# Loading w_mod first, three of its row tiles in full fp32, and the rest of it on Pool's queue

## The chip, the cores and the metric

The kernel runs on one core of one Trainium2 chip. The metric is the time of one execution in microseconds, as the device reports it. Before the change it is 1837.02 us, the median of three runs (1834.33 to 1839.08).

## The reference, cut to what matters

One layer of a diffusion backbone over 1024 latent tokens and 256 context tokens of width 1024. Per sample, a conditioning vector gives six vectors of modulation; the tokens are normalised, scaled and shifted, and projected by one large matrix:

```python
def adaln_params(cond, w_mod, b_mod):
    m = jax.nn.silu(cond) @ w_mod + b_mod            # (1024,) @ (1024, 6144)
    return jnp.split(m[..., None, :], N_MOD, axis=-1)
...
    sh1, sc1, g1, sh2, sc2, g2 = adaln_params(c, w_mod[l], b_mod[l])
    csh1, csc1, cg1, csh2, csc2, cg2 = adaln_params(c_ctx, w_mod[l], b_mod[l])
    hx = modulate(rms_norm(x, norm1_g[l]), sh1, sc1)       # h * (1 + scale) + shift
    hc = modulate(rms_norm(ctx, norm1_g[l]), csh1, csc1)
    y_x, y_c = token_mix(hx, hc, w_in[l], ...)             # begins with hx @ w_in and hc @ w_in
    x = x + g1 * y_x
    x = x + g2 * expert_choice_moe(modulate(rms_norm(x, norm2_g[l]), sh2, sc2), ...)
```

Token mixing (a recurrent branch, an attention branch, gates) and sixteen experts follow. All data are fp32.

## The kernel before, in words

**Precision.** Most products are made of three matmuls in the type fp32r, which keeps fewer bits of a number: an operand is written as `hi` (rounded by ACT, `nc.scalar.copy`, line 92) and `lo` (the rest, subtracted by DVE, line 93), and hi*hi + hi*lo + lo*hi are summed (`mm3g`, lines 172 to 179). `split` is this pair of instructions.

**The opening stage (lines 242 to 369)** computes shift and scale of the first norm and modulates the tokens. The first 2048 of w_mod's 6144 columns come in eight row tiles `wm` of 128 x 2048 (1 MB); `silu(c)` and `silu(c_ctx)` stand in columns, `s_col`, and as hi and lo in `s4` (four columns). For each tile k: split into `w2` (ACT, then DVE), then eight matmuls of 512 columns into four sums `pm` (line 322). Then the sums are copied to `m2`, turned into columns (`ptc`, line 339), and with b_mod and norm1_g become `modc` and the scale `sv` (lines 342 to 345).

Beside that the ten token tiles (0 and 1 are context; 2 to 5 are half 0 of x, 6 to 9 half 1) are loaded (`xload`), normalised (`normalise`: ACT squares and sums, Pool computes the inverse root, lines 85 and 87, DVE or Pool multiplies, line 296 or 294) and turned by PE (`turn_in`, line 303; DVE and ACT copy the result, line 304). The tuples XA, XB, XC say behind which tile k a token tile is loaded, normalised and turned; 9 means behind the loop. `modulate` multiplies and adds per row of channels (line 350; DVE for even k, Pool for odd) and splits the result into HC (context) and HX[0], HX[1] (the halves).

**The projection.** `ws` is a stream of w_in's column tiles of 256 columns (`wload`, lines 156 to 166: load to `raw`, split into `whi` and `wlo`); two of them can stand ready. `natural` multiplies one column tile by the token tiles asked for, 24 matmuls of 256 columns each (lines 176 to 178), and ACT copies each result to `stg` (three buffers), from which SP's queue stores it (`staged`, line 70). In the opening stage column 0 is multiplied with tiles 0 and 1, then with 2 to 4 (XD = 3) with the turns of half 1 between them, and behind the modulation of half 1 with 5 to 9. Columns 1 to 20 follow. The remaining 4096 columns of w_mod are loaded in sixteen tiles of 1 MB (line 490, two buffers) and summed by DVE, each times its number of `s_col` (`macc`, lines 493 and 495); this is written in the loop over columns 3 to 6, and the scheduler moves it up to columns 0 to 3. The sums end in a product in plain fp32 (line 518), whose result is needed much later.

**What sets the order.** PE executes in the order in which the program is written. For the other engines a scheduler orders instructions by priority; each engine then executes its queue strictly in order, and a waiting instruction holds all behind it. DMAs are instructions of the engine that issues them (SP, ACT or Pool) and wait in its queue for the buffers that they fill. Buffers are shared by tag: before, the eight w_mod tiles go round the four buffers whi0, wlo0, whi1, wlo1.

Of the kernel before, what the change touches and what calls it, by code (L numbers as in the profile page):

```python
# [9 lines left out]
F32 = mybir.dt.float32  # L10
F32R = mybir.dt.float32r
# [10 lines left out]
D = 1024  # L22
# [12 lines left out]
def dram(a, off, dims):  # L35
    return bass.AP(tensor=a.tensor, offset=a.offset + off, ap=[list(d) for d in dims])
# [9 lines left out]
def _layer(tc, nc, top, A, out):  # L46
# [43 lines left out]
    def split(hi, lo, src, eng=None):  # L90

        nc.scalar.copy(hi, src)  # L92
        (eng or nc.vector).tensor_tensor(lo, src, hi.bitcast(F32), op=OP.subtract)  # L93
# [93 lines left out]
    hxp = top.enter_context(ExitStack())  # L187
    hx_pool = hxp.enter_context(mkpool(name="hx", bufs=1))

    HX = [[hx_pool.tile([128, 8, 512], F32R, name="hx", tag=f"hx0{i}") for i in range(2)]]  # L190
    hcp = top.enter_context(ExitStack())
    hc_pool = hcp.enter_context(mkpool("right", name="hc", bufs=1))
    HC = [hc_pool.tile([128, 8, CT], F32R, name=f"hc{i}") for i in range(2)]
# [11 lines left out]
    def natural(hi, lo, emit, tiles):  # L205

        n = hi.shape[2]
        for t in tiles:
            h = HC if t < 2 else HX[(t - 2) // 4]
            o = (t if t < 2 else (t - 2) % 4) * 128  # L210
            p = pjt()
            yield from mm3g(p[:, :n], (lambda k: h[0][:, k, o:o + 128], lambda k: h[1][:, k, o:o + 128]),
                            (lambda k: hi[:, k], lambda k: lo[:, k]), 8)
            emit(t, p[:, :n])
            fill.flushed()
# [11 lines left out]
    def dense(gen):  # L227
        for _ in gen:
            pass
# [12 lines left out]
    with ExitStack() as st:  # L242
# [5 lines left out]
        X = {}  # L248

        def xload(t):  # L250
            X[t] = pool.tile([128, D], F32, name="xt", tag="xt", bufs=4)
            nc.sync.dma_start(X[t], A["ctx"][0, t * 128:(t + 1) * 128] if t < 2 else A["x"][0, (t - 2) * 128:(t - 1) * 128])


        XA, XB, XC = (0, 0, 1, 1, 2, 2, 9, 9, 9, 9), (1, 1, 2, 2, 3, 4, 9, 9, 9, 9), (2, 3, 4, 5, 6, 6, 9, 9, 9, 9)
        XD = 3
        wm = []
        for k in range(8):
            w = wp.tile([128, 2048], F32, name="wm", tag=("whi0", "wlo0", "whi1", "wlo1")[k % 4])
            nc.sync.dma_start(w, dram(A["w_mod"], k * 128 * 6144, [[6144, 128], [1, 2048]]))  # L260
            wm.append(w)
            for t in range(10):
                if XA[t] == k:
                    xload(t)
        n1 = pool.tile([8, 128], F32, name="n1")
        nc.scalar.dma_start(n1, A["norm1_g"].rearrange("a (k p) -> (a k) p", p=128))
        bm = pool.tile([16, 128], F32, name="bm")
# [15 lines left out]
        nc.vector.tensor_copy(n1c, pt[:, 16:40])  # L283

        XN = {}
        MP, NP = (1, 3, 5, 7), (1, 3, 5, 7, 9)

        def normalise(t):
            ss = pool.tile([128, 1], F32, name="ss", bufs=3)
            scr = pool.tile([128, D], F32, name="scr", tag="scr", bufs=2)  # L290
            nc.scalar.activation(scr, X[t], AF.Square, accum_out=ss)
            r = rsqrt(pool, ss, 1, 1.0 / D, "rx")
            if t in NP:
                nc.gpsimd.tensor_scalar(scr, X[t], r, 1.0, op0=OP.mult, op1=OP.mult)
            else:
                nc.vector.tensor_scalar(scr, X[t], r, None, op0=OP.mult)
            XN[t] = scr
# [13 lines left out]
        def turn_in(t):  # L311
            if t < 2:
                transpose_in(t, xnc, t * 128)
            else:
                transpose_in(t, halves[(t - 2) // 4], (t - 2) % 4 * 128)

        for k in range(8):
            w2 = hx_pool.tile([128, 2, 2048], F32R, name="wm2", tag="hx1%d" % (k % 2))
            split(w2[:, 0], w2[:, 1], wm[k])
            for j in range(4):  # L320
                for i in range(2):
                    nc.tensor.matmul(pm[j], s4[:, k], w2[:, i, j * 512:(j + 1) * 512],
                                     start=(k == 0 and i == 0), stop=(k == 7 and i == 1))
            for t in range(10):
                if XB[t] == k:
                    normalise(t)
                if XC[t] == k:
                    turn_in(t)
        HX.append([hx_pool.tile([128, 8, 512], F32R, name="hx", tag=f"hx1{i}") for i in range(2)])
        ws.load(0)  # L330
        for t in range(10):
            if XA[t] > 7:
                xload(t)
        m2 = pool.tile([4, 2048], F32, name="m2")
        for j in range(4):
            (nc.scalar.copy if j % 2 else nc.vector.tensor_copy)(m2[:, j * 512:(j + 1) * 512], pm[j])
        pc = ps.tile([128, 512], F32, name="ptc", tag="tp", bufs=2)
        for j in range(16):
# [5 lines left out]
        sv = pool.tile([128, 8, 2], F32, name="sv")  # L344
        nc.vector.scalar_tensor_tensor(sv, modc[:, 8:], 1.0, n1c[:, :8, None].to_broadcast([128, 8, 2]),
                                       op0=OP.add, op1=OP.mult)

        def modulate(xt, dst, o, n, j):
            for k in range(8):
                (nc.gpsimd if k in MP else nc.vector).tensor_scalar(xt[:, k], xt[:, k], sv[:, k, j:j + 1], modc[:, k, j:j + 1], op0=OP.mult, op1=OP.add)  # L350
                split(dst[0][:, k, o:o + n], dst[1][:, k, o:o + n], xt[:, k])

        modulate(xnc, HC, 0, CT, 1)
        for t in range(10):
            if XB[t] > 7:
                normalise(t)
        for t in range(6):
            if XC[t] > 7:
                turn_in(t)
        (w,), ahead = ws.next()  # L360
        dense(natural(*w, to_v(0), range(2)))
        modulate(halves[0], HX[0], 0, 512, 0)
        for t in range(2, 6):
            if t - 2 < XD:
                dense(natural(*w, to_v(0), [t]))
# [23 lines left out]
    with ExitStack() as st:  # L389
# [26 lines left out]
        for i, n in enumerate(("c_cos", "c_sin")):  # L416
            a = pool.tile([128, 8, 64], F32, name="rot", bufs=1, tag="rot%d" % i)
            nc.scalar.dma_start(a, A[n].rearrange("(t p) c -> p t c", p=128))
            (nc.gpsimd, nc.vector)[i].tensor_tensor(a, a, rows[:, i:i + 1].to_broadcast([128, 8, 64]), op=OP.mult)
            rot.append(a)  # L420
        akv = pool.tile([128, 10, 256], F32, name="akv", bufs=1)

# [55 lines left out]
        for hp in range(2):  # L478
            for d in range(2):
                (w,), ahead = ws.next()  # L480
                ahead()
                for m in range(2):
                    dense(transposed(*w, m, to_fk(hp * 2 + m, d), True))
                    i = 4 * hp + 2 * d + m
                    for _ in range((i >= KQ) + (i > 9 - KQ)):
                        next(kturn, None)
                for k in range(4 * hp + 2 * d, 4 * hp + 2 * d + 2):
                    for j in range(2):
                        wm = pool.tile([128, 2048], F32, name="wm", tag="wm")
                        nc.sync.dma_start(wm, dram(A["w_mod"], k * 128 * 6144 + 2048 + j * 2048, [[6144, 128], [1, 2048]]))  # L490
                        a = acc[:, j * 2048:(j + 1) * 2048]
                        if k == 0:
                            nc.vector.tensor_scalar(a, wm, s_col[:, k, 0:1], None, op0=OP.mult)
                        else:
                            nc.vector.scalar_tensor_tensor(a, wm, s_col[:, k, 0:1], a, op0=OP.mult, op1=OP.add)
# [1015 lines left out]
```

## Time and profile before

| | |
|---|---|
| median of three runs | 1837.02 us (1834.33 to 1839.08) |
| the profiled execution | 1835.68 us |
| its span, first to last instruction | 1833.9 us |
| mean granted clock of TensorE | 0.978 |
| busy: PE, PEld, DVE, ACT, POOL | 94%, 79%, 72%, 54%, 12% |
| moved by DMA | 383.87 MB, 209 GB/s in the mean |

The span is shorter than the execution's time by 1.8 us, which lie before the first and behind the last instruction. PE is the matmul unit, PEld its weight load, which runs beside it. A busy share is a mean over stages with different limits; the granted clock is 1.00 at full speed and 0.50 at half. A row of the timeline gives the start and the length of one instruction or of a merged run (x8), and in brackets how long its engine had been idle and what ended that.

### The profile page before, as it was taken

The page shows a single profiled execution, that of the slowest core. Times are in us where ns is not written, and L with a number is a line of the kernel's source. Part 1 is how long each engine was busy: PE and PEld are TensorE (multiplying, and loading weights), DVE is VectorE, ACT ScalarE, POOL GpSimd, SP SyncE. Part 2 cuts the span into 40 slices and gives each one's busy share as a digit, 9 for nine tenths or more (in the row PEclk, how much of TensorE's full clock was granted, in tenths as well). Part 3 has the DMA queues.
Part 4 walks back from the last instruction along what each step waited for, and adds up shares of the span by engine and source line. Part 5 has one row for each costly group of instructions (what it writes and reads, how often), then busy time and mean ns, then how long its engine had stood idle before and what let it go on. Part 6 is the DMA issues. An engine that isn't in the chain of part 4 may idle for free. (4 is left out here: it accounts for less than half of the span.)

```text
span 1833.9 us, 26101 instructions
## 1 busy us (share of the span) xinstructions
PE 1728.6 (94%) x9819; PEld 1451.0 (79%) x9820; DVE 1325.1 (72%) x2016; ACT 981.6 (54%) x1608; POOL 225.1 (12%) x218
## 2 busy tenths in 40 slices
PE   5899999999999899999999999849999999999996
PEld 2799887899988678787777899838888888887774
DVE  5756322876756567777887664469999999999897
ACT  6522331332322367777767432237777777776665
POOL 3400001020000201111100010030010011001103
PEclk8899999999999999999999999969999999999998
DMA  8386445353332311101222676569999999999962
GB/s 321 98 290 238 155 144 186 128 159 106 128 113 81 119 51 34 53 24 58 94 91 99 223 269 230 176 238 356 380 380 375 382 385 369 383 384 381 357 244 95
DMA packets 206319, 383.87 MB, mean 209 GB/s; under 512 B 17488, under 2 KB 65568, under 8 KB 202864
## 3 DMA queue, kind: packets, MB, share of 16 engines
q1 hardware_dynamic: 194944, 360.92, 55.2%
q0 software_dynamic: 4832, 19.34, 3.9%
q10 hardware_dynamic: 6416, 1.94, 0.4%
q8 instruction: 77, 1.26, 0.3%
q14 instruction: 50, 0.41, 0.1%
HBM read 323.02 MB, written 59.13 MB: 208 GB/s over the span
## 5 line engine op out<-in xcount | busy, mean ns | idle before, releaser
L93 DVE TENSOR_TENSOR elo<-eraw,ehi 128x1024 fp32r<-128x1024 f32 x378 | 452.1, 1220 | 22.4 <-ACT ehi L92 14.9
L92 ACT CAST ehi<-eraw 128x1024 fp32r<-128x1024 f32 x384 | 383.7, 1048 | 86.5 <-PE pgu L178 48.4
L177 PE MATMUL pgu<-elo,xeT 128*128 128x512 f32 x512 | 203.5, 397 | 2.8 <-DVE elo L93 2.4
L176 PE MATMUL pgu<-ehi,xeT 128*128 128x512 f32 x512 | 205.3, 401 | 0.2 <-ACT xeT L92 0.2
L178 PE MATMUL pgu<-ehi,xeT 128*128 128x512 f32 x512 | 201.6, 394 | 0.0
L176 PE MATMUL pj<-hx,whi 128*128 128x512 f32 x448 | 185.7, 414 | 6.2 <-ACT stg L567 4.2
L178 PE MATMUL pj<-hx,wlo 128*128 128x512 f32 x448 | 176.4, 394 | 0.0
L177 PE MATMUL pj<-hx,whi 128*128 128x512 f32 x448 | 175.9, 393 | 0.0
L797 ACT ACTIVATE p<-s,m,qsc 128x512 f32<-128x512 f32 (+1 forms) x192 | 134.2, 711 | 18.8 <-DVE m L794 18.6
L790 DVE TENSOR_REDUCE m<-s 128x1 f32<-128x512 f32 (+1 forms) x192 | 104.2, 595 | 43.8 <-PE s L788 43.6
L176 PE MATMUL pj<-whi,hx 128*128 128x256 f32 x448 | 130.9, 292 | 3.8 <-DVE stg L541 1.9
L92 ACT CAST pT<-ptp 128x512 fp32r<-128x512 f32 x160 | 92.4, 593 | 75.4 <-PE ptp L806 75.2
L178 PE MATMUL pj<-whi,hx 128*128 128x256 f32 x448 | 128.1, 286 | 1.4 <-DVE hx L93 1.3
L93 DVE TENSOR_TENSOR pT<-ptp,pT 128x512 fp32r<-128x512 f32 x160 | 108.0, 684 | 26.5 <-ACT pT L92 25.6
L177 PE MATMUL pj<-wlo,hx 128*128 128x256 f32 x448 | 127.2, 284 | 0.0
L177 PEld LDWEIGHTS pgu<-elo,xeT 128*128 128x128 f32 x512 | 96.2, 188 | 28.6 <-DVE elo L93 8.1
L178 PEld LDWEIGHTS pgu<-ehi,xeT 128*128 128x128 f32 x512 | 96.1, 188 | 23.1 <-DVE xeT L93 0.4
L176 PEld LDWEIGHTS pgu<-ehi,xeT 128*128 128x128 f32 x512 | 96.7, 189 | 22.1 <-ACT xeT L92 0.5
L176 PE MATMUL pye<-ehi,hdT 128*128 128x512 f32 x256 | 105.3, 411 | 0.0
L816 PE MATMUL pv<-pT,vs 128*128 128x512 f32 x320 | 102.9, 404 | 1.8 <-DVE pT L93 1.5
L177 PE MATMUL pye<-elo,hdT 128*128 128x512 f32 x256 | 102.3, 400 | 1.2 <-DVE elo L93 1.2
L176 PEld LDWEIGHTS pj<-hx,whi 128*128 128x128 f32 x448 | 85.2, 190 | 21.1 <-ACT stg L567 5.1
(367 smaller groups left out, 3788.7 us busy)
## 6 DMA issues: line engine op xcount, KB each, us to landing
eraw<-in_w_exp_gate SPq DMA_DIRECT2D x64, 1024.0 KB, 10.0
eraw<-in_w_exp_up SPq DMA_DIRECT2D x64, 1024.0 KB, 9.5
eraw<-in_w_exp_down SPq DMA_DIRECT2D x64, 1024.0 KB, 10.0
wm<-in_w_mod SPq DMA_DIRECT2D x24, 1024.0 KB, 6.3
raw<-in_w_in SPq DMA_DIRECT2D x21, 1024.0 KB, 6.7
sFK<-sg SPq DMA_DIRECT2D x32, 256.0 KB, 2.3
sGT<-stg SPq DMA_DIRECT2D x32, 256.0 KB, 2.0
F<-sFK SPq DMA_DIRECT2D x8, 640.0 KB, 4.2
```

What stands on the lines that cost most here:

```text
L92: nc.scalar.copy(hi, src)
L93: (eng or nc.vector).tensor_tensor(lo, src, hi.bitcast(F32), op=OP.subtract)
L176: nc.tensor.matmul(p, a[0](k), b[0](k), start=s, stop=False)
L177: nc.tensor.matmul(p, a[0](k), b[1](k), start=False, stop=False)
L178: nc.tensor.matmul(p, a[1](k), b[0](k), start=False, stop=e)
L790: nc.vector.tensor_reduce(m[:, a:a + 1], s, axis=AX.X, op=OP.max)
L797: nc.scalar.activation(p, ss[a], AF.Exp, bias=m[:, 7:8], scale=sc, accum_out=SU[t, g][:, a, h:h + 1])
L816: nc.tensor.matmul(PV[t, g].rearrange("p a b -> p (a b)"), VS[:, g, j], hl[i], start=(j == 0 and i == 0), stop=(j == 9 and i == 1))
```

## The change

There are four edits. The eight w_mod tiles get a buffer each (the four of before and HX[0]'s two, which are not yet in use and hold two tiles each) and are loaded in one go, with only the two context tiles between them; token tiles 2 to 9 are loaded later, into six buffers instead of four, and normalised and turned at other places (XB and XC are now tables by k). Tiles 1, 3 and 5 are not split: PE multiplies them with `s_col` as they are, in fp32, into the first two rows of the same sums. What follows the sums up to `sv` has a higher priority for the scheduler, and `dummies` puts twelve matmuls on old data, whose result nobody reads, behind the sums. `modulate` treats half 0 in two pieces of 256 tokens, and of eight channel rows four are multiplied by DVE, two by ACT, two by Pool. Last, the sixteen later loads of w_mod are issued by Pool instead of SP, and Pool makes both `rot` products.

```diff
--- before.py
+++ after.py
@@ -187,7 +187,7 @@
...
-    HX = [[hx_pool.tile([128, 8, 512], F32R, name="hx", tag=f"hx0{i}") for i in range(2)]]
+    HX = []
...
@@ -248,20 +248,20 @@
         X = {}
         def xload(t):
-            X[t] = pool.tile([128, D], F32, name="xt", tag="xt", bufs=4)
+            X[t] = pool.tile([128, D], F32, name="xt", tag="xt", bufs=6)
             nc.sync.dma_start(X[t], A["ctx"][0, t * 128:(t + 1) * 128] if t < 2 else A["x"][0, (t - 2) * 128:(t - 1) * 128])
-        XA, XB, XC = (0, 0, 1, 1, 2, 2, 9, 9, 9, 9), (1, 1, 2, 2, 3, 4, 9, 9, 9, 9), (2, 3, 4, 5, 6, 6, 9, 9, 9, 9)
-        XD = 3
-        wm = []
+        XB, XC = {0: [0], 1: [1], 5: [2], 6: [3]}, {2: [0], 3: [1], 6: [2, 3]}
+        FULL, XD, DM = (1, 3, 5), 3, 12
+        wm = [wp.tile([128, 2048], F32, name="wm", tag=n) for n in ("whi0", "wlo0", "whi1", "wlo1")]
+        for i in range(2):
+            w = hx_pool.tile([128, 2, 2048], F32, name="wm4", tag="hx0%d" % i)
+            wm += [w[:, 0], w[:, 1]]
         for k in range(8):
-            w = wp.tile([128, 2048], F32, name="wm", tag=("whi0", "wlo0", "whi1", "wlo1")[k % 4])
-            nc.sync.dma_start(w, dram(A["w_mod"], k * 128 * 6144, [[6144, 128], [1, 2048]]))
-            wm.append(w)
-            for t in range(10):
-                if XA[t] == k:
-                    xload(t)
+            nc.sync.dma_start(wm[k], dram(A["w_mod"], k * 128 * 6144, [[6144, 128], [1, 2048]]))
+            if k in (0, 1):
+                xload(k)
...
@@ -283,7 +283,7 @@
...
-        MP, NP = (1, 3, 5, 7), (1, 3, 5, 7, 9)
+        ME, NP = "vsvsvpvp", (1, 3, 5, 7, 9)
...
@@ -314,24 +314,36 @@
             else:
                 transpose_in(t, halves[(t - 2) // 4], (t - 2) % 4 * 128)
+        def dummies(n):
+
+            p = ps.tile([128, 512], F32, name="pw", tag="tp", bufs=2)
+            for _ in range(n):
+                nc.tensor.matmul(p, w2[:, 0, :128], w2[:, 0, :512], start=True, stop=True)
+
         for k in range(8):
-            w2 = hx_pool.tile([128, 2, 2048], F32R, name="wm2", tag="hx1%d" % (k % 2))
-            split(w2[:, 0], w2[:, 1], wm[k])
-            for j in range(4):
-                for i in range(2):
-                    nc.tensor.matmul(pm[j], s4[:, k], w2[:, i, j * 512:(j + 1) * 512],
-                                     start=(k == 0 and i == 0), stop=(k == 7 and i == 1))
-            for t in range(10):
-                if XB[t] == k:
-                    normalise(t)
-                if XC[t] == k:
-                    turn_in(t)
-        HX.append([hx_pool.tile([128, 8, 512], F32R, name="hx", tag=f"hx1{i}") for i in range(2)])
-        ws.load(0)
-        for t in range(10):
-            if XA[t] > 7:
-                xload(t)
-        m2 = pool.tile([4, 2048], F32, name="m2")
+            if k in FULL:
+
+                for j in range(4):
+                    nc.tensor.matmul(pm[j][:2], s_col[:, k], wm[k][:, j * 512:(j + 1) * 512], start=False, stop=False)
+            else:
+                w2 = hx_pool.tile([128, 2, 2048], F32R, name="wm2", tag="hx1%d" % (k % 4 // 2))
+                split(w2[:, 0], w2[:, 1], wm[k])
+                for j in range(4):
+                    for i in range(2):
+                        nc.tensor.matmul(pm[j], s4[:, k], w2[:, i, j * 512:(j + 1) * 512],
+                                         start=(k == 0 and i == 0), stop=(k == 7 and i == 1))
+            if k in (4, 6):
+                if k == 6:
+                    ws.load(0)
+                for t in range(k - 2, k):
+                    xload(t)
+            for t in XB.get(k, ()):
+                normalise(t)
+            for t in XC.get(k, ()):
+                turn_in(t)
+        hp = tc.high_priority(offset=60)
+        hp.__enter__()
+        m2 = hx_pool.tile([4, 2048], F32, name="m2", tag="hx00")
         for j in range(4):
             (nc.scalar.copy if j % 2 else nc.vector.tensor_copy)(m2[:, j * 512:(j + 1) * 512], pm[j])
...
@@ -344,22 +356,33 @@
...
+        hp.__exit__(None, None, None)
         def modulate(xt, dst, o, n, j):
             for k in range(8):
-                (nc.gpsimd if k in MP else nc.vector).tensor_scalar(xt[:, k], xt[:, k], sv[:, k, j:j + 1], modc[:, k, j:j + 1], op0=OP.mult, op1=OP.add)
-                split(dst[0][:, k, o:o + n], dst[1][:, k, o:o + n], xt[:, k])
-
+                sk, ok, x = sv[:, k, j:j + 1], modc[:, k, j:j + 1], xt[:, k, o:o + n]
+                if ME[k] == "s":
+                    nc.scalar.activation(x, x, AF.Identity, bias=ok, scale=sk)
+                else:
+                    (nc.gpsimd if ME[k] == "p" else nc.vector).tensor_scalar(x, x, sk, ok, op0=OP.mult, op1=OP.add)
+                split(dst[0][:, k, o:o + n], dst[1][:, k, o:o + n], x)
+
+        dummies(DM)
         modulate(xnc, HC, 0, CT, 1)
-        for t in range(10):
-            if XB[t] > 7:
-                normalise(t)
-        for t in range(6):
-            if XC[t] > 7:
-                turn_in(t)
+        for h in range(2):
+            HX.append([hx_pool.tile([128, 8, 512], F32R, name="hx", tag=f"hx{h}{i}") for i in range(2)])
         (w,), ahead = ws.next()
-        dense(natural(*w, to_v(0), range(2)))
-        modulate(halves[0], HX[0], 0, 512, 0)
+        for t in (4, 5):
+            normalise(t)
+        for t in range(6, 10):
+            xload(t)
+        modulate(halves[0], HX[0], 0, 256, 0)
+        for t in range(2):
+            dense(natural(*w, to_v(0), [t]))
+            turn_in(4 + t)
+        modulate(halves[0], HX[0], 256, 256, 0)
+        for t in range(6, 10):
+            normalise(t)
         for t in range(2, 6):
             if t - 2 < XD:
                 dense(natural(*w, to_v(0), [t]))
@@ -416,7 +439,7 @@
         for i, n in enumerate(("c_cos", "c_sin")):
             a = pool.tile([128, 8, 64], F32, name="rot", bufs=1, tag="rot%d" % i)
             nc.scalar.dma_start(a, A[n].rearrange("(t p) c -> p t c", p=128))
-            (nc.gpsimd, nc.vector)[i].tensor_tensor(a, a, rows[:, i:i + 1].to_broadcast([128, 8, 64]), op=OP.mult)
+            nc.gpsimd.tensor_tensor(a, a, rows[:, i:i + 1].to_broadcast([128, 8, 64]), op=OP.mult)
             rot.append(a)
         akv = pool.tile([128, 10, 256], F32, name="akv", bufs=1)
@@ -487,7 +510,7 @@
                 for k in range(4 * hp + 2 * d, 4 * hp + 2 * d + 2):
                     for j in range(2):
                         wm = pool.tile([128, 2048], F32, name="wm", tag="wm")
-                        nc.sync.dma_start(wm, dram(A["w_mod"], k * 128 * 6144 + 2048 + j * 2048, [[6144, 128], [1, 2048]]))
+                        nc.gpsimd.dma_start(wm, dram(A["w_mod"], k * 128 * 6144 + 2048 + j * 2048, [[6144, 128], [1, 2048]]))
                         a = acc[:, j * 2048:(j + 1) * 2048]
                         if k == 0:
                             nc.vector.tensor_scalar(a, wm, s_col[:, k, 0:1], None, op0=OP.mult)
```

On ACT, around the last three w_mod tiles, the queue of before reads (`wm_305`, `wm_328` and `wm_363` are the rounded tiles 5, 6 and 7, L291 the square of a token, L304 the copy of a turned one):

```order
L92 CAST wm_305<-wm 128x2048
L291 ACTIVATE scr,ss<-xt 128x1024
L304 COPY xnc<-ptx 128x4x128
L92 CAST wm_328<-wm 128x2048
L291 ACTIVATE scr,ss<-xt 128x1024
L304 COPY xh<-ptx 128x4x128
L92 CAST wm_363<-wm 128x2048
```

and the queue of the changed kernel (`wm_224`, `wm_251` and `wm_304` are the rounded tiles 4, 6 and 7, `raw` the first tile of w_in):

```order
L92 CAST wm_224<-wm_113 128x2048
L304 COPY xnc<-ptx 128x4x128 x2
L92 CAST wm_251<-wm_114 128x2048
L291 ACTIVATE scr,ss<-xt 128x1024
L92 CAST wm_304<-wm_114 128x2048
L291 ACTIVATE scr,ss<-xt 128x1024
L304 COPY xh<-ptx 128x4x128
L92 CAST whi<-raw 128x2048
```

Tile 5 is gone from it, both context copies stand ahead of tile 6, and the square of token 3 stands behind tile 7.

On PE, the changed kernel has between the last matmuls of tile 6 (`wm_251`) and the first of the projection (`pj`) these rows; `ptx` are the turns of tokens 2 and 3, `ptc` that of the sums, `pw` the extra matmuls:

```order
L333 MATMUL pm_150<-wm_251,s_142 4x512 x2
L303 MATMUL ptx<-ident,scr 128x128 x16
L333 MATMUL pm_147<-wm_304,s_142 4x512 x2
L333 MATMUL pm_148<-wm_304,s_142 4x512 x2
L333 MATMUL pm_149<-wm_304,s_142 4x512 x2
L333 MATMUL pm_150<-wm_304,s_142 4x512 x2
L351 MATMUL ptc<-ident,m_315 128x4 x16
L321 MATMUL pw<-wm_304 128x512 x12
L176 MATMUL pj<-whi,hc_86 128x256
```

Before, the same sixteen turns stood there for tokens 4 and 5, and the row `pw` did not exist.

On Pool, the changed kernel has behind the modulation of half 1 (L367) these rows, down to the inverse root for the keys (`kss`, `kr`):

```order
L367 TENSOR_SCALAR xh<-xh,sv,modc 128x512 x2
L513 DMA wm<-in_w_mod 128x2048 x2
L535 MEMSET sel 128x64
L513 DMA wm<-in_w_mod 128x2048
L442 TENSOR_TENSOR rot<-rot,rows 128x512 x2
L513 DMA wm<-in_w_mod 128x2048
L536 MEMSET sel 128x8
L513 DMA wm<-in_w_mod 128x2048 x12
L461 TENSOR_SCALAR kss<-kss 128x20
L462 TENSOR_TENSOR kr__1473<-kss,mhalf 128x20
```

The sixteen loads stood in SP's queue before, between the stores of `stg`; Pool had one of the rot products and no DMA there.

## Rows read from the trace of the kernel before

**Rows 1.** Stretches: PE, PEld, DVE, ACT, POOL busy, granted clock, DMA share, GB/s
```profile
19.50:21.00 1.50, 0.69 (x2) 0.08 (x1) 0.99 (x1) 0.48 (x1) 0.00 (x0) 0.50 1.08 448
...
20.00:30.00 10.00, 5.92 (x20) 2.21 (x21) 5.65 (x4) 5.32 (x5) 1.30 (x2) 0.67 1.00 413
...
120.00:140.00 20.00, 20.00 (x168) 19.84 (x167) 14.50 (x13) 5.81 (x10) 0.00 (x0) 1.00 0.87 304
```

**Rows 2.** Timeline, ACT: start, us, operation [idle before <-what ended it]
```profile
7.91 1.90 ACT L92 CAST wm<-wm 128x2048 fp32r<-128x2048 f32 x1 [1.53 <-DMA wm<-in_w_mod]
...
12.97 1.90 ACT L92 CAST wm<-wm 128x2048 fp32r<-128x2048 f32 x1 [1.07 <-DMA wm<-in_w_mod]
```

**Rows 3.** Timeline, all engines, 9 to 52 us
```profile
9.84 2.29 DVE L93 TENSOR_TENSOR wm<-wm,wm 128x2048 fp32r<-128x2048 f32 x1 [3.12 <-ACT wm L92]
...
12.19 3.29 PE L322 MATMUL pm<-wm,s 128*4 128x512 f32 x8 [1.74 <-DVE wm L93]
...
25.29 1.03 PE L303 MATMUL ptx<-ident,scr 128*128 128x128 f32 x8
...
32.73 2.09 PE L322 MATMUL pm<-wm,s 128*4 128x512 f32 x8
...
47.20 2.99 PE L322 MATMUL pm<-wm,s 128*4 128x512 f32 x8
...
51.75 0.63 DVE L345 SCALAR_TENSOR_TENSOR sv<-modc,n1c 128x16 f32<-128x16 f32 x1
```

**Rows 4.** Timeline, half 1 of the tokens, 78 to 87 us
```profile
78.28 2.31 DVE L350 TENSOR_SCALAR xh<-xh,sv,modc 128x512 f32<-128x512 f32 x3
...
78.35 6.13 POOL L350 TENSOR_SCALAR xh<-xh,sv,modc 128x512 f32<-128x512 f32 x4 [2.31 <-DVE xh L304]
...
86.91 0.58 PE L178 MATMUL pj<-whi,hx 128*128 128x256 f32 x1 [0.22 <-DVE hx L93]
```

**Rows 5.** Line 518, fp32: ns min/median/max, first and last start
```profile
L518 PE MATMUL pr<-macc,sel x16: 593/593/596, 292.5 to 298.9; 128*8 128x512 f32 x16
```

**Rows 6.** Timeline, Pool's steps for a token, pieces of tokens, a tile's end
```profile
28.11 0.74 POOL L85 TENSOR_SCALAR rxm<-ss 128x1 f32<-128x1 f32 x1 [12.97 <-ACT scr L291]
...
36.41 0.55 POOL L87 TENSOR_TENSOR rx<-rxm,mhalf 128x1 f32<-128x1 f32 x1
...
37.07 1.12 POOL L294 TENSOR_SCALAR scr<-xt,rx 128x1024 f32<-128x1024 f32 x1
...
53.82 2.48 DVE L93 TENSOR_TENSOR hc<-xnc,hc 128x256 fp32r<-128x256 f32 x6
...
60.14 0.58 PE L178 MATMUL pj<-whi,hc 128*128 128x256 f32 x1
...
61.07 1.95 DVE L93 TENSOR_TENSOR hx<-xh,hx 128x512 fp32r<-128x512 f32 x3
```

**Rows 7.** Groups by shape, 0 to 100 us: busy us, mean ns
```profile
L291 ACT ACTIVATE scr<-xt 128x1024 f32<-128x1024 f32 x10 | 10.6, 1059 | 1.0 <-PE ptx L303 1.0
...
L92 ACT CAST hx<-xh 128x512 fp32r<-128x512 f32 x16 | 9.2, 617 | 4.0 <-POOL xh L350 3.9
...
L92 ACT CAST hc<-xnc 128x256 fp32r<-128x256 f32 x8 | 2.8, 401 | 3.2 <-POOL xnc L350 3.2
```

**Rows 8.** Waits: who waited for what: us, times, longest
```profile
ACT stg L69 <- DMA sV<-stg: 12.8, 4, 3.5
```

**Rows 9.** Waits of PE, 95 to 300 us
```profile
PE pj L176 <- ACT stg L69: 1.1, 1, 1.1
```

**Rows 10.** Line 725, Pool's large load: ns, starts; landing in us
```profile
L725 POOL DMA_DIRECT2D kT<-sKT x2: 617/641/665, 518.0 to 591.0; - x2
...
DMA to landing us min/median/max: 6.2/6.9/7.6
```

**Rows 11.** Tile macc: the sums' instruction, ns
```profile
L495 DVE SCALAR_TENSOR_TENSOR macc<-wm,s_col,macc x14: 2303/2351/2354, 107.2 to 169.5; 128x2048 f32<-128x2048 f32 x14
```

**Rows 12.** Timeline, DVE: the rot product and what it waited for
```profile
101.07 0.81 DVE L419 TENSOR_TENSOR rot<-rot,rows 128x512 f32<-128x512 f32 x1 [6.52 <-DMA rot<-in_c_sin]
```

## The prediction

> **What bounds the kernel now.** I read the page first: PE is busy for 94% of the span, so time is to be had only where PE waits or runs slowly. The table by stretches shows where [rows 1]: PE is busy 5.92 us of 10 at a granted clock of 0.67 in 20 to 30 us, and 20.00 of 20 at 1.00 in 120 to 140. Between 95 and 300 us the table of PE's waits has one entry, 1.1 us [rows 9]. So what the change gives in the first 90 us is kept to the end, and what it takes there is paid.
>
> Next I read the timeline. The first stage is a chain: eight row tiles of w_mod arrive, ACT rounds each (1.90 us), DVE subtracts the rest (2.29 us), PE multiplies. ACT waits for the loads of tile 0 until 7.91 and of tile 1 until 12.97 [rows 2]; between them came tile 1 (1 MB) and two token tiles (0.5 MB each), so a MB takes 5.06 / 2 = 2.53 us. Tile 7 is multiplied only from 47.20 to 50.2, and the scale sv is ready at 51.75 + 0.63 = 52.4 [rows 3]. The second landmark is the last modulated piece of half 1: PE takes it at 86.91 [rows 4], 34.5 us behind sv.
>
> **The change, step by step.** All times that follow are estimates: durations from rows of before, placed in the new order of each engine.
>
> *Loads.* With only two context tiles between them and a buffer of its own for each, w_mod tiles 0 to 7 land at 7.9, 11.7, 15.5, 18.0, 20.6, 23.1, 25.6 and 28.1 us; tokens 2 and 3 at 29.4 and 30.7, the first w_in tile at 33.2. SP's waits for freed buffers go here.
>
> *Three tiles in full fp32.* This takes 3 x (1.90 ACT + 2.29 DVE) off those engines. On PE the nearest row is L518, also fp32 with 512 columns: eight matmuls of the program are 16 records from 292.5 to 298.9 [rows 5], so with the last one's 0.43 they take 0.85 us each, 3.4 for a tile, against 2.09 for a split one [rows 3]. At half clock, which split tile 0 shows (3.29 us), the fp32 tile would be 6.8. So the clock decides much here, and I had to choose. In before it is 0.50 in 19.5 to 21 us, where PE is busy 0.69 of 1.5 us [rows 1]; in after tile 1 has landed at 11.7 and follows tile 0 without a gap. I take full clock from about 17 us on.
>
> *Chain to the scale.* PE: tile 0 until 15.5; tile 1 until 19.5 (0.6 for the slow start); tile 2, whose rest is ready at 15.5 + 1.9 + 2.3 = 19.7, until 21.8; token 0's eight transposes 1.0; tile 3 until 26.2; token 1's transposes until 27.2; tile 4 until 29.3; tile 5 until 32.7. ACT copies token 1 behind these transposes and only then rounds tile 6 (27.8 to 29.7); DVE has its rest at 32.0, PE multiplies from 32.7 to 34.8. Tile 7 goes to the same buffer as tile 6, so ACT rounds it from 34.8 to 36.7 and then squares token 3 (1.06 and 0.2 for its sum); Pool's three steps take 0.74 + 0.55 + 1.12 [rows 6]: 40.3. Token 3's transposes stand on PE ahead of tile 7: 41.3, then tile 7 until 43.4. DVE has a copy of token 3 (0.7) and the 2.29 us rest of the first w_in tile ahead of its two copies of the sums (0.7 each): 45.1. Sixteen small transposes 0.6, three small operations 1.1: sv at 46.8. That is 5.6 us earlier; what keeps it from more is that tokens 2 and 3 still stand between tiles 6 and 7.
>
> *Twelve extra matmuls* on old data run where PE would wait for modulated tokens: 3.29 / 8 = 0.41 each at half clock, 4.9 in all, or 2.5 at full. From 45.7 they end at 48.2 or 50.6; the first modulated piece is there at about 48. I cost them at 0; where the clock is low, 2.6.
>
> *Modulation.* Half 0 goes in two pieces of 256 tokens: ACT's rounding costs 0.40 for 256 against 0.62 for 512 [rows 7], DVE's rest 2.48 / 6 = 0.41 against 1.95 / 3 = 0.65 [rows 6]. For this half that is 16 x 0.40 - 8 x 0.62 = 1.4 us more on ACT and 16 x 0.41 - 8 x 0.65 = 1.4 on DVE. Two of eight multiplications go to ACT; no row shows that operation. The bounds are a 256 cast, 0.40, and the 1024 square, 1.06 [rows 7]; I take 0.45, near the row of its own size. Pool, whose four for half 1 take 6.13 us [rows 4], has two. In return tile 0 of the projection is supplied some 5.6 us behind sv (eight pieces of 0.4 + 0.4 on DVE, shared with those of half 0) instead of 8.3 (tile 0's last matmul, at 60.14 [rows 6], ends 60.7). Then come tiles 1 to 4 at 24 x 20 / 168 = 2.9 [rows 1] and six turns of tokens at 1.0, and one wait of 2.8, since ACT squares token 7 only behind a row of roundings: 46.8 + 5.6 + 17.6 + 2.8 = 72.8. Half 1 took 86.9 - 78.3 = 8.6 us [rows 4] and with less on Pool takes some 8.3: 81.1, which is 34.3 us behind sv against 34.5: 0.2 gained. Tiles 6 to 9 are as before.
>
> *The rest of w_mod on Pool's queue.* In before ACT waits 12.8 us for the stores sV, which share SP's queue with the 1 MB loads [rows 8]; 1.1 reaches PE [rows 9]. I take that as gained (bounds 0 and 1.1). The sixteen loads now go in Pool's order. Behind the third stand the two rot products, which wait for ACT's loads: until 101.07 in before [rows 12], so 96 now, and with two products 99. Behind the last loads stand kss and kr. DVE, in its order, has the split of w_in column 3 behind the tenth sum and that of column 4 behind the sixteenth. With two buffers a load takes half of issue 0.64, landing 6.9 (kT, Pool's only large load) and sum 2.35 [rows 10, 11]: 4.9 us. Bounds by the shortest and longest landing: 4.6 and 5.3. Thirteen loads from 99: 163, split of column 4 at 165. PE wants it when column 3 ends: column 0 ends three tiles and some slow clock behind half 1 (81.1 + 10.5 = 92), two columns at 10 x 2.9 and one at 26 follow: 175. So there are 10 us of cover and no cost; above (175 - 2 - 99) / 13 = 5.7 us a load each further 0.1 costs 1.3.
>
> The Trainium skill speaks against this part: SBUF — State Buffer, section "SBUF: two separate sides", says that a DMA issued by GpSimd needs descriptors that GpSimd writes, and that VectorE locks it out while it runs in a two-port mode. No run here shows such loads beside a busy DVE: kT's were issued at 518 and 591 us. By the rule they would land later than 6.9; that is the third rival.
>
> *Sum.* 5.6 + 0.2 + 1.1 = 6.9 us off the profiled execution's 1835.7 (span 1833.9): 1828.8. The median of before, 1837.0, lies 1.3 higher; on that footing 1830.1. I forecast 1830.
>
> **Rivals.**
> - *It packs better than I place it.* If token 3 is turned while PE still multiplies tile 6, sv follows the last load: 28.1 + 1.9 + 2.3 + 3.0 + 52.4 - 50.2 = 37.5 at best. For it: loads and ACT would allow it. Against: tile 7's rounding waits for tile 6. Half way, sv at 42: 1825; with 4 us from Pool's lighter share 1821. 17%.
> - *Modulation or a longer slow start eats it.* ACT has some 31 us of work in the 34 us behind sv, and each wait between ACT and DVE counts. Three to five us more: 1833 to 1835, no change. 22%.
> - *Slower: Pool's loads come too late.* At 7.5 us a load the sixteenth sum is at 99 + 97 = 196, the split at 198 against 175: PE stands 23 us: 1853. It decides from 5.7 us a load, and from 6.6 the kernel is slower by over 0.3%. For it: no row has these loads under load. 10%.
> - *Slower: PE stays at half clock while it multiplies w_mod.* Tiles 1, 3 and 5 take 6.8, the split ones 3.3: tile 6 ends near 48 instead of 34.8 and sv comes at 60, 8 behind before: 1837 + 8 - 1.3 = 1844. For it: the 0.67 of 20 to 30 us. Against: no gaps on PE now. 6%.
>
> **How the numbers follow.** The forecast itself has 45%, its own range 1826 to 1834. A measurement of this kernel tells 0.3%, 5.5 us, from no change: faster is below 1831.5, slower above 1842.5. Faster: 17 + 39 of the 45 + 2 of the 22 = 0.58. Slower: 9 + 3 of the two last = 0.12. Same: 0.30. Eight in ten: 1820 to 1840, which leaves out the two slow rivals and the edges.
>
> **What would show it.** Right: tile 7 landed by 29 us; the fp32 matmuls of L327 at 0.43 a record and a granted clock of 1.00 from 17 to 34; sv at 46 to 48; half 1's last piece at 81; PE without a wait for wlo behind 90 us; ACT's wait for sV gone. Wrong: 0.50 in 20 to 35; w_mod loads on Pool's queue landing in over 8 us, DVE waiting for them in its sums (L516 and L518 of the changed kernel) and PE for wlo; or sv before 43.

## The result, and the profile after

The changed kernel takes 1846.32 us, the median of six runs (1844.98 to 1851.89); the kernel before, also over six runs, 1837.94. The ratio is 1.0053, 95% interval [1.0040, 1.0066]: slower by 8.4 us. I had forecast 1830 and a range of 1820 to 1840; sign and range were both wrong. Executions of one kernel scatter by some us (the kernel before: 1831.51 to 1843.96 over 32 of them), so below the medians give the prices, and a single trace shows the places.

The profiled execution after took 1845.8 us (span 1844.0, granted clock 0.98). I read it as I read before, from the front. The opening stage did most of what was forecast. Granted clock by stretch (columns as in [rows 1]: the third number from the end of a line), then PE's timeline, where line 327 is the fp32 product and 333 the split one:

```profile
19.50:21.00 1.50, 1.35 (x6) 0.51 (x7) 0.10 (x1) 0.58 (x1) 0.00 (x0) 1.00 0.98 410
20.00:30.00 10.00, 10.00 (x43) 3.72 (x41) 4.27 (x4) 5.60 (x5) 0.00 (x0) 1.00 1.01 413
40.00:50.00 10.00, 9.61 (x46) 6.33 (x46) 7.56 (x13) 6.07 (x14) 3.55 (x7) 0.69 0.52 159
```
```profile
12.12 3.15 PE L333 MATMUL pm<-wm,s 128*4 128x512 f32 x7 [1.74 <-DVE wm L93]
15.20 3.72 PE L327 MATMUL pm<-wm,s_col 128*2 128x512 f32 x8
...
22.24 3.60 PE L327 MATMUL pm<-wm,s_col 128*2 128x512 f32 x8
...
40.39 1.97 PE L303 MATMUL ptx<-ident,scr 128*128 128x128 f32 x8 [5.34 <-POOL scr L294]
42.01 3.76 PE L333 MATMUL pm<-wm,s 128*4 128x512 f32 x8
...
46.98 3.03 PE L321 MATMUL pw<-wm 128*128 128x512 f32 x12
```

Against [rows 1] PE has 10.00 us of work in 20 to 30 at full clock, where it had 5.92 at 0.67. The wait of 5.34 for token 3 ahead of tile 7 is the one that the forecast had placed at 40.3. Behind it the clock is lower (0.69 in 40 to 50), and tile 7 takes 3.76, where tile 6 took 2.02. The scale follows on DVE, and the last piece of half 1 comes at 77.83 + 4.88 = 82.7 where before it was 86.9 [rows 4]:

```profile
47.53 0.20 DVE L357 SCALAR_TENSOR_TENSOR sv<-modc,n1c 128x16 f32<-128x16 f32 x1
...
77.83 4.88 DVE L93 TENSOR_TENSOR hx<-xh,hx 128x512 fp32r<-128x512 f32 x8
```

sv is there at 47.7, before at 52.4 [rows 3]. That lead is one trace against one: e2 below, whose opening is before's, has sv at 49.1, and the ten traces with the new opening and its fp32 tiles lie between 46.8 and 47.7. Where [rows 9] had one wait of PE, of 1.1 us, there are now five in three groups (us in total, times, longest), with a lower clock behind the three long ones; in before the same five stretches had 1.00. (The second block has PE's columns alone: busy time, clock, DMA share, GB/s.)

```profile
PE pj L176 <- ACT sg L491: 4.4, 1, 4.4
PE pj L176 <- ACT stg L69: 4.1, 3, 3.2
PE pj L176 <- ACT akv L447: 2.7, 1, 2.7
```
```profile
100.00:110.00 10.00, 6.82 (x38) 0.71 0.94 317
110.00:120.00 10.00, 10.00 (x82) 0.95 0.75 249
130.00:140.00 10.00, 7.31 (x56) 0.92 0.69 228
140.00:150.00 10.00, 10.00 (x78) 0.91 0.95 316
180.00:190.00 10.00, 7.41 (x25) 0.83 0.22 79
```

The books close with these rows. ACT's last copy of column 0 is at 95.37, in before at 98.65: 3.3 us ahead. The product of the sums on PE, a good landmark since PE has no wait between 190 and 300 us in either trace, starts at

```profile
L541 PE MATMUL pr<-macc,sel x16: 592/592/596, 303.5 to 309.9; 128*8 128x512 f32 x16
```

against 292.5 [rows 5]: 11.0 us behind. So 14.3 us went between 95 and 303. The long waits are 3.2 + 2.7 + 4.4 = 10.3, less before's 1.1; the lost clock, by stretch PE's busy time times what the clock lacks to 1.00, is 6.82 x 0.29 + 10.00 x 0.05 + 7.31 x 0.08 + 10.00 x 0.09 + 7.41 x 0.17 = 5.2. Sum 14.4, a short wait of 0.55 at 95.8 left out. The wait for the store has 5.7 of it (3.2 and 2.5 of clock), the two behind `akv` and `sg`, explained next, 9.8 (7.1 and 2.7). From the landmark to the end both need the same: 1540.5 and 1541.4.

Who made PE wait? ACT copies each finished product away (`stg` for columns 0 and 1, `akv` for column 2, `sg` for column 3). Its timeline shows two instructions that themselves wait for DVE with finished products behind them, and one copy that waits for a store:

```profile
104.53 0.65 ACT L69 COPY stg<-pj 128x256 f32<-128x256 f32 x2 [6.71 <-DMA sV<-stg]
...
136.25 0.22 ACT L429 ACTIVATE lc<-lc 128x16 f32<-128x16 f32 x1 [4.65 <-DVE lc L428]
136.37 0.63 ACT L447 COPY akv<-pj 128x256 f32<-128x256 f32 x2
...
180.42 1.14 ACT L92 CAST kd<-kr 128x512 fp32r<-128x512 f32 x2 [9.39 <-DVE kr L469]
181.47 1.62 ACT L491 ACTIVATE sg<-pj 128x512 f32<-128x512 f32 x4
```

`lc` is a small softmax of 16 numbers per partition; its exp (line 429) stands on ACT ahead of column 2's copies. `kd` is the keys' rounding; it stands ahead of the sigmoids `sg` of column 3. On DVE what they need comes behind the sums of w_mod, nearly all of which wait for their loads:

```profile
133.31 2.35 DVE L518 SCALAR_TENSOR_TENSOR macc<-wm,s_col,macc 128x2048 f32<-128x2048 f32 x1 [1.51 <-DMA wm<-in_w_mod]
135.57 0.17 DVE L424 COPY lc<-pl 128x16 f32<-128x16 f32 x1
...
163.78 2.35 DVE L518 SCALAR_TENSOR_TENSOR macc<-wm,s_col,macc 128x2048 f32<-128x2048 f32 x1 [0.78 <-DMA wm<-in_w_mod]
166.05 2.28 DVE L93 TENSOR_TENSOR wlo<-raw,whi 128x2048 fp32r<-128x2048 f32 x1
168.25 1.48 DVE L459 TENSOR_REDUCE kss<-kr 128x20 f32<-128x1280 f32 x1
```

133.31 is the ninth sum and 163.78 the sixteenth. In before eight stood ahead of lc, the sixteenth stood behind kss, and kss ran at 162.59:

```profile
128.54 2.35 DVE L495 SCALAR_TENSOR_TENSOR macc<-wm,s_col,macc 128x2048 f32<-128x2048 f32 x1 [0.76 <-DMA wm<-in_w_mod]
130.81 0.17 DVE L401 COPY lc<-pl 128x16 f32<-128x16 f32 x1
131.49 0.22 ACT L406 ACTIVATE lc<-lc 128x16 f32<-128x16 f32 x1 [0.19 <-DVE lc L405]
...
162.59 1.48 DVE L436 TENSOR_REDUCE kss<-kr 128x20 f32<-128x1280 f32 x1
169.54 2.34 DVE L495 SCALAR_TENSOR_TENSOR macc<-wm,s_col,macc 128x2048 f32<-128x2048 f32 x1
176.90 1.14 ACT L92 CAST kd<-kr 128x512 fp32r<-128x512 f32 x2 [5.18 <-DVE kr L446]
```

The order of ACT changed with it: the kd cast stood behind four 512 sigmoids, now behind two.

```
before, ACT                                after, ACT
L468 ACTIVATE sg<-pj 128x256 x2            L491 ACTIVATE sg<-pj 128x256 x2
L468 ACTIVATE sg<-pj 128x512 x4            L491 ACTIVATE sg<-pj 128x512 x2
L92 CAST kd<-kr 128x512 x2                 L92 CAST kd<-kr 128x512 x2
                                           L491 ACTIVATE sg<-pj 128x512 x2
```

Theory 1: the moved loads cost it, by these places in the queues. Theory 2: the new opening costs it. Theory 3: loads from Pool's queue cost it by themselves, by contention, which means that transfers slow each other.

### The profile page after: what moved, and what is told of

Same layout as the page of the kernel before. It is cut to its first block, busy times and chain, and to the rows that moved or that the text cites. A ratio compares the mean times of both kernels' runs of the same rounds, so it can differ in the third digit from the quotient of the medians.

```text
span 1844.0 us, 26150 instructions
## 1 busy us (share of the span) xinstructions
PE 1734.7 (94%) x9831; PEld 1454.3 (79%) x9832; DVE 1316.7 (71%) x2024; ACT 980.1 (53%) x1621; POOL 226.4 (12%) x231
## 5 line engine op out<-in xcount | busy, mean ns | idle before, releaser
L177 PE MATMUL pye<-elo,hdT 128*128 128x512 f32 x256 | 102.3, 399 | 1.2 <-DVE elo L93 1.2
## 6 DMA issues: line engine op xcount, KB each, us to landing
wm<-in_w_mod SPq DMA_DIRECT2D x8, 1024.0 KB, 13.7
```

Source lines behind the costliest of these rows:

```text
L177: nc.tensor.matmul(p, a[0](k), b[1](k), start=False, stop=False)
```

## The experiments

Behind each time stand its ratio to the kernel before and the 95% interval. The runs came in three groups (e; f1, f2, f3 and f6; f5 and g), with medians of the kernel before of 1838.23, 1837.77 and 1837.91, so times of different groups can be compared to within half a us and the scatter.

**e1: the loads back on SP.**

```diff
-                        nc.gpsimd.dma_start(wm, dram(A["w_mod"], ...
+                        nc.sync.dma_start(wm, dram(A["w_mod"], ...
```

> The changed kernel with the sixteen later loads of w_mod back on SP's queue; the opening stage stays as changed. Theory 1 (the moved loads cost it: DVE takes nine sums before lc and sixteen before kss, and PE stands 2.7 us behind the exp of lc and 4.4 us behind kd, plus the slow clock after each): DVE is back to eight and fifteen sums, PE has no wait over 1.5 us between 95 and 300 us, the time is the forecast's 1830 to 1834. Theory 2 (the new opening stage costs it, by leaving less slack at its end): 1843 to 1848, the waits at 137 and 183 us stay. Theory 3 (contention of Pool's loads for the DMA engines costs it, not the order): 1830 to 1834 too, told from theory 1 by e3.

Measured: 1833.68 us, ratio to before 0.9976 [0.9963, 0.9990]. Theory 2 falls. But of the opening's lead little is left: PE still waits three times for sV copies (1.8 in all), 0.6 behind akv and 1.8 behind sg, longer than the 1.5 that I expected at most, and in the profiled execution, whose 1839.0 lies 5 above the median, the landmark is at 292.2 against 292.5.

**e2: the moved loads alone, on the kernel before** (the `rot` product stays where it was).

```diff
-                        nc.sync.dma_start(wm, dram(A["w_mod"], ...
+                        nc.gpsimd.dma_start(wm, dram(A["w_mod"], ...
```

> The kernel before with the sixteen later loads of w_mod on Pool's queue and nothing else. Theories 1 and 3: slower by what the changed kernel lost beyond the opening's gain, 10 to 15 us: 1847 to 1853, with PE waits of 2 to 5 us behind the exp of lc and behind kd. Theory 2: 1836 to 1840, no change.

Measured: 1848.59, 1.0053 [1.0033, 1.0074]: about the same loss without the new opening (10.4 us against before; between e1 and the changed kernel it is 12.6), at the same two places:

```profile
PE pj L176 <- ACT akv L424: 4.2, 1, 4.2
PE pj L176 <- ACT sg L468: 3.6, 1, 3.6
```

Two waits for sV copies, 2.1 in all, come to them. So the loss sits in this one line. e3 and e4 ask how.

**e3: Pool's queue, DVE's old order.** The later sums read a copy of `s_col` that DVE makes behind `lb1` (the softmax's last step) or behind kss, so they cannot stand ahead of those:

```diff
+        nc.vector.scalar_tensor_tensor(sl[0], lb1[...], 0.0, s_col, op0=OP.mult, op1=OP.add)
...
+            nc.vector.scalar_tensor_tensor(sl[1], ss[...], 0.0, s_col, op0=OP.mult, op1=OP.add)
...
+                        sk = s_col if 2 * k + j < 8 else sl[2 * k + j > 14]
...
```

> The changed kernel, loads on Pool's queue, with DVE's order put back: sums 9 to 15 read a copy of the scale column that DVE makes behind lb1, the sixteenth one that it makes behind kss, so that eight sums stand before lc and fifteen before kss; two small DVE operations more. Theory 1: the waits at 137 us (2.7) and at 183 us (4.4) go or fall under 1 us each, and with the clock after them 8 to 11 us come back: 1835 to 1838. Theory 3 (contention): the order matters little, 1843 to 1847, and the loads take as long. If only the wait at 92 to 108 us mattered: no change either.

Measured: 1844.09, 1.0031 [1.0019, 1.0043]. A miss for theory 1 as I had put it: 2 us of 8 to 11. The wait behind akv even grew to 3.8, that behind sg fell to 1.9:

```profile
PE pj L176 <- ACT akv L449: 3.8, 1, 3.8
PE pj L176 <- ACT stg L69: 2.4, 2, 1.9
PE pj L176 <- ACT sg L494: 1.9, 1, 1.9
```

Its eighth sum started only at 132.08, where before's started at 128.54. So it is not only how many sums stand ahead, but when they come.

**e4: the small loads early.** SP loads k_norm_g's rows and c_sin behind the first w_in tile and two token tiles, instead of ACT at 83 to 92 us:

```diff
+                if k == 6:
+                    gain_rows(rows, "k_norm_g")
+                    nc.sync.dma_start(rot0, A["c_sin"].rearrange("(t p) c -> p t c", p=128))
...
```

> The changed kernel with k_norm_g's rows and c_sin loaded by SP in the first stage instead of by ACT at 83 to 92 us; one product of rot moves to Pool's modulation. Theory 1 for the first wait (copies of ACT stand behind its DMA issues, and SP's stores of sV behind the landing of these rows): the PE waits of 92 to 108 us (0.35, 0.55, 3.18) fall below 1 us in sum and the clock of 100 to 110 rises from 0.71 to 0.95 or more: 4 to 6 us come back, 1840 to 1843. Rival: Pool's 1 MB loads delay whatever lands there, the sV stores wait all the same: 1844 to 1848.

Measured: 1844.46, 1.0032 [1.0020, 1.0043]. The waits of 92 to 108 us are gone and the clock of 90 to 110 is 1.00, as expected; column 0 ends at 91.73 (after: 95.37) and column 1 at 120.39, 7.4 us ahead of before's 127.81. And then:

```profile
PE pj L176 <- ACT sg L497: 5.4, 1, 5.4
PE pj L176 <- ACT akv L453: 4.7, 1, 4.7
```

lc runs at 130.26, the last akv copy at 155.88 (before: 156.86): 6.4 of the 7.4 us are handed back there, and the next wait takes the rest and more. That gave theory 1b: lc and kss are fixed in time by the train of sums, and a lead of PE ends at the first of them.

**f1 and f2: the train earlier.** The first two loads go straight into the accumulator, so loads three and four need no sum to end first; f1 on e4, f2 on the changed kernel alone.

```diff
+                        a = acc[:, j * 2048:(j + 1) * 2048]
-                        wm = pool.tile([128, 2048], F32, name="wm", tag="wm")
+                        wm = pool.tile([128, 2048], F32, name="wm", tag="wm") if k else a
...
```

> e4 (k_norm_g's rows and c_sin loaded early, later w_mod on Pool's queue) with the first two 1 MB loads of the sums going straight into the accumulator and scaled in place, so that loads three and four need no sum to end first. Theory 1b (the sums are a train paced by its two buffers and loads; lc behind the ninth and kss behind the sixteenth sum are fixed in time by it, so whatever PE has gained before is given back there): the train is 5 to 9 us earlier, the PE waits behind akv (4.7) and sg (5.4) fall below 2 us each, the L547 matmuls start at 287 to 292 instead of 299.3, and the time is 1832 to 1837. Theory 3 (contention): the loads only slow each other, the ninth and sixteenth sums stand where they stood (127.6, 159.1) and the time is 1842 to 1846.

> The changed kernel with the first two 1 MB loads of the sums going straight into the accumulator, nothing else. Theory 1b: ninth and sixteenth sums 5 to 9 us earlier than 133.3 and 163.8; PE's waits behind akv (2.7) and sg (4.4) fall below 1 us each, the waits of 92 to 108 us stay: 1835 to 1840. Theory 3: 1843 to 1848.

f1: 1840.17, 1.0011 [1.0001, 1.0021], 4.3 us below e4. The ninth and sixteenth sums start at 121.72 and 152.77 instead of 127.59 and 159.11, and the wait behind akv is gone. That behind sg stayed, against expectation (6.3, in e4 5.4), with kss already at 157.25. ACT's timeline shows why: kd waits 11.37 us for its data, and the sigmoids that PE needs stand behind it.

```profile
156.97 1.08 ACT L497 ACTIVATE sg<-pj 128x512 f32<-128x512 f32 x2 [3.01 <-PE pj L178]
169.42 1.14 ACT L92 CAST kd<-kr 128x512 fp32r<-128x512 f32 x2 [11.37 <-DVE kr L475]
170.46 1.62 ACT L497 ACTIVATE sg<-pj 128x512 f32<-128x512 f32 x4
```

f2: 1847.21, 1.0052 [1.0036, 1.0068], no gain, a miss. Its sums came 4.9 us earlier, and the waits of 92 to 108 us vanished too (the first two loads are issued from 77.9 on, ACT's small ones from 83.6), so PE came to lc 7.2 us earlier (last copy of column 1 at 120.90 instead of 128.12) and waited 5.0 there instead of 2.7. One of the three remedies alone only moves the wait.

**f5: Pool's queue with all three.** f1 with e3's order, which also puts kd behind four 512 sigmoids instead of two.

> Loads on Pool's queue as in the changed kernel, with the order of e3 (eight sums before lc, fifteen before kss, and with them ACT's kd cast behind the third pair of 512 sigmoids instead of the second), the small loads of e4 and the early train of f1. Theory 1c (what costs is the place of lc and kd in the queues of DVE and ACT, not the queue that issues the loads): PE's waits behind akv and sg together below 1.5 us, the sums of macc on PE start at 285 to 288, the time is f6's, 1829 to 1833. Theory 3 (loads from Pool's queue cost by themselves): f1's 1838 to 1842 stays.

Measured: 1832.59, 0.9976 [0.9966, 0.9986], 7.6 below f1 (6.4 by the ratios) by the order alone. kd comes no earlier than in f1; it only stands one pair later:

```profile
162.64 1.09 ACT L500 ACTIVATE sg<-pj 128x512 f32<-128x512 f32 x2 [4.35 <-PE pj L178]
170.54 1.14 ACT L92 CAST kd<-kr 128x512 fp32r<-128x512 f32 x2 [6.81 <-DVE kr L478]
```

Of PE's waits from 90 to 300 us one is left, of 1.3, and the landmark is at 286.1. Theory 3 falls as the cause of the loss: with the same loads on the same queue the kernel is 13.7 us faster than the changed one. Nor do these loads land clearly later from Pool's queue: the median is 5.6 to 7.0 us in the seven traces that have them there, and 5.2 to 7.6 in the seven that have them on SP's (six of these up to 6.1). What is left open is the 2.7 us by which f5 lies above f6 below, whose intervals overlap.

**f3 and f6: the train earlier on SP's queue**, f3 on e1, f6 with e4's early loads as well.

> e1 (later w_mod on SP's queue) with the first two loads going straight into the accumulator. Theory 1b: e1 gave back most of the opening's 5 us at the same two places (PE waits 0.6 and 1.8 and three of 0.9 and less behind sV copies); with the train earlier 2 to 4 us more come back: 1829 to 1832. Theory 3: as e1, 1833 to 1835, or slower where the earlier loads hold up the sV stores on SP.

> f3 with k_norm_g's rows and c_sin loaded early by SP as in e4. Theory 1b: PE's column 0 ends at 92 as in e4 and the gain of 7 us over the kernel before is kept at the two places: 1827 to 1831, the L547 matmuls start at 284 to 288. If SP's in-order queue is what binds (sV stores behind 1 MB loads): PE waits of 1 to 3 us behind ACT's copies, 1832 to 1836.

f3: 1835.44, 0.9986 [0.9976, 0.9996], no gain over e1: the waits for sV copies (1.9) remained, and the ninth sum started at 131.92 as in e1 (132.09); in SP's queue the third and fourth loads stand behind sV stores. f6: 1829.94, 0.9962 [0.9948, 0.9976], the best version, 7.8 us faster than before. On SP's queue DVE and ACT have before's order again (eight sums ahead of lc, kd behind four sigmoids), as in e1. From 90 to 300 us PE has no wait at all:

```profile
90.00:110.00 20.00, 20.00 (x170) 1.00 0.88 331
110.00:300.00 190.00, 190.00 (x1122) 1.00 0.55 185
```
```profile
L547 PE MATMUL pr<-macc,sel x16: 592/592/596, 285.1 to 291.5; 128*8 128x512 f32 x16
```

**g4, g2, g3: what the opening is worth.** g4 is the kernel before with f6's two later edits; g2 is f6 with `FULL = ()`; g3 is f6 with `DM = 0`.

> The kernel before (old opening, loads on SP) with the two edits of f6: small loads early by SP, first two loads into the accumulator. If the opening gives f6 its gain: PE's column 0 ends 5 to 6 us later than in f6 (97 to 98), the sums of macc start at 290 to 293, 1836 to 1838. If the two edits alone do it: 1829 to 1832.

> f6 with no tile of w_mod in full fp32, all eight split. ACT and DVE have 3 x 1.9 and 3 x 2.3 us more ahead of the scale; part of it fits into their idle time. sv at 49 to 52 instead of 47.5, time 1831.5 to 1834. If fp32 gives nothing beside the loads' new order: sv at 47 to 48 and 1829 to 1831.

> f6 without the twelve extra matmuls. If they keep the clock up: granted clock below 0.8 in some of 48 to 70 us where f6 has 1.00, time 1831 to 1834. If they do nothing: 1829 to 1831, and if they delay the first tiles: below 1829.

g4: 1840.46, 1.0013 [0.9999, 1.0027], sv at 54.1, column 0 ends at 101.86: the two edits alone give nothing, the opening gives 10.5 us on that footing, more than I expected. The small loads do not stand at quite the same place in the old opening, and sv and column 0 are later there than in before (52.4, 98.65), so part of the 10.5 may be theirs. g2: 1839.44, 1.0011 [1.0001, 1.0022], sv at

```profile
L370 DVE SCALAR_TENSOR_TENSOR sv<-modc,n1c x1: 174/174/174, 56.1 to 56.1; 128x16 f32<-128x16 f32 x1
```

so sv comes 8.9 us and the end 9.5 us later than in f6, more than I expected. This is not the price of the three fp32 tiles alone. The split tiles share two buffers by `k % 4 // 2`, so with all eight split, tiles 0 and 1, 2 and 3, and so on, have the same one, and ACT waits for PE to be done with a tile before it rounds the next: 13.5 us in four waits, where f6 has one of 3.9 (tiles 6 and 7) and g4, which alternates by `k % 2`, one of 2.1. What fp32 is worth with the buffers sorted again was not run. In time g2 and g4 are the same.

g3: 1830.51, 0.9967 [0.9956, 0.9978], as f6. Without the twelve matmuls the clock is lower (0.71 below, 1.00 in f6's same stretch), but PE has slack there (it waits for modulated pieces) and column 0 ends at 92.06 instead of 91.74:

```profile
50.00:60.00 10.00, 9.46 (x60) 0.71 0.06 18
```

## Why the prediction was wrong, step by step

- *Loads, fp32 tiles, chain to the scale:* right up to token 3's turn, and by luck behind it. The clock was 1.00 from 17 to 34 us, and an fp32 tile took 3.60 to 3.72 for a forecast 3.4. But behind its wait of 5.34 PE ran at half clock (0.50 from 41 to 46 us), so tile 7 ended at 45.8 for 43.4, 2.4 late. What made up for it is that DVE had finished the rest of the w_in tile meanwhile and the sums were copied as they came, which the forecast had put behind tile 7 with 1.7. So sv came at 47.7 for 46.8.
- *Modulation:* right in kind, 0.7 short: 35.0 us behind sv instead of 34.3. ACT's multiplication took 0.60 for my 0.45; the token 7 wait was 3.2 for 2.8.
- *Twelve extra matmuls at nothing:* right, as far as g3 shows it on f6.
- *1.1 us gained from the sV wait:* wrong. Pool's first loads were issued at 83, together with ACT's small ones; k_norm_g's rows landed in 10.5 us instead of 7.0, SP's sV stores, by the profile, waited 6.6 for them (before 0.7; why a store waits for rows that it does not read, the profile does not show), and ACT's wait for sV was still 6.7 ([rows 8]: 12.8), of which 3.2 reached PE in one piece.

```profile
SPq L70 <- DMA rows<-in_k_norm_g: 6.6, 1, 6.6
```

- *Pool's loads, "10 us of cover and no cost":* the step that failed. The waits behind `akv` and `sg` and the clock behind them cost 9.8 us where the sum has nothing. Its own numbers held, with two errors that cancel (the rot products ended at 102.3 for 99): from the third to the sixteenth sum 4.57 us a load (forecast 4.9), the last sum at 163.8 (163), the split of column 4 at 166.1 (165) for a deadline of 175, and PE never waited for it. The Trainium skill's rule in SBUF — State Buffer, section "SBUF: two separate sides", by which VectorE's two-port modes would hold up such loads, is not tested here, since no trace shows in which mode a sum ran. No delay shows: the loads landed in

```profile
DMA to landing us min/median/max: 5.1/7.0/11.4
```

with the median of kT's [rows 10] within 0.1 us. The failure was the list of victims. I named the splits of columns 3 and 4 as what waits behind the sums. The instructions with the near deadline were lc, whose exp on ACT has column 2's copies behind it, and kss, whose kd has column 3's sigmoids behind it. Their cover was not 10 us but about nothing: in before the exp already waited 0.2 us for lc, and kd stood one pair of sigmoids further back, which was just enough. The new order of DVE and ACT is fixed before the kernel runs, so it could have been read beforehand.
- *Rivals:* "slower: Pool's loads come too late" named the right line and the wrong mechanism: it needed 5.7 us a load, and the loss came at 4.57. The half clock of the last rival came, behind tile 0, for tile 7 alone.

## What to carry to other kernels

When a load changes its queue, the scheduler may also change the order on the engines that use it: list on each of them what now stands behind the moved instructions and take the earliest deadline, also of tiny operations (a softmax of 16 columns cost 2.7 us and the clock behind it). A lead won early is kept only up to the next instruction that something else fixes in time; here, on Pool's queue, it took three remedies together to carry 7 us past two such places, and each alone gave 2 us or nothing. A run that takes a part away can also upset something that the part had made room for (g2): look at the waits before its time is taken as the part's price. A wait that vanishes in the trace while the time stays is the sign of it: look for the next wait, which has grown.

## What was not expected of the hardware

Each of the three waits of 2.7 to 4.4 us on an otherwise dense PE was followed by some us at a lower clock. Behind the first, the granted clock was 0.50 from 104.9 to 111, and matmuls that take 0.28 us at full clock took 0.41. So 10.3 us of waits cost 15.5. Waits of 1.1 us (before), 1.3 (f5) and 1.8 (e1) left the clock of their slices of 10 us at 1.00.

Small loads took longer in the changed kernel: c_cos landed in 12.1 us, where in before c_sin took 9.1. How long one issue takes on ACT's queue varies much, too. The columns are ns min/median/max and start, the changed kernel's row first:

```profile
L441 ACTq DMA_DIRECT2D rot<-in_c_sin x1: 3012/3012/3012, 88.6 to 88.6; - x1
```
```profile
L418 ACTq DMA_DIRECT2D rot<-in_c_sin x1: 381/381/381, 92.0 to 92.0; - x1
```

That the 1 MB loads of Pool's queue do this is not shown: the same issue took 0.38 in e3 too, which has them, and 3.28 in e2, and the issue of b_mod's row behind it took 2.55 in the changed kernel and 3.64 in before. What holds an issue back, the traces do not show.
